# First value blocks of a hybrid attention step multiplied before their norm is known, first loads reordered, the sample's output block last but one

## The chip, the cores and the metric

The kernel runs on one core of a Trainium2 chip. Its time is the device time of one execution in microseconds, and the median of several runs counts. The engines named below are TensorE (PE in the profile; its weight loads are PEld), VectorE (DVE), ScalarE (ACT), GpSimd (POOL) and SyncE (SP), whose queue issues the transfers. A line number such as L213 is the line of the kernel file of before.

## The reference

One layer of a streaming encoder, for 1024 prompt frames and 32 frames of a running stream (the sample), each of 1024 channels. What matters here is how it starts and how it ends:

```python
def rmsnorm(x, g):
    xf = x.astype(F32)
    y = xf * lax.rsqrt(jnp.mean(xf * xf, axis=-1, keepdims=True) + EPS) * g.astype(F32)
    return y.astype(x.dtype)

def in_proj(xn, w_in, gla_w_a2, gla_b_a):
    u = xn @ w_in          # 1024 -> 10256 columns
    gq, gk, gv, gr, gg, dq, dk, dv, dg, ma, mb = jnp.split(u, IN_SPLITS, axis=-1)
    ...

def out_merge(x, o_gla, o_diff, gg, dg, ma, mb, ...):
    ...
    merged = jax.nn.sigmoid(ma) * (yg @ w_proj_gla) + jax.nn.sigmoid(mb) * (yd @ w_proj_diff)
    return x + rmsnorm(merged @ w_out, post_norm_g)
```

Between the two stand a gated linear attention of 4 heads and a differential attention of 8 heads, which the change doesn't touch. The factor of the root mean square is one number per frame, so it can be applied to the rows of x or to the rows of a product x @ w.

## The kernel before, in words

Every float32 product is made of three products of rounded parts: each operand is split into a high part (a copy rounded to the type fp32r, on ScalarE) and a low part (the operand less the high part, on VectorE, or on GpSimd for the projection weights), and high by high, low by high and high by low are added up in PSUM.

The normalized input stays in SBUF for the whole input projection: `X` holds 1024 channels (8 groups `k` of 128 partitions, kept as one tile of 6 groups and one of 2) by high and low part by 1056 frames. It is filled block by block; blocks 0 to 7 are 128 prompt frames each, block 8 is the sample's 32. For one block:

- `norm_square` (L196) loads the block twice, by rows (`xn`) and by columns (`xr`), takes the sum of squares of each row on ScalarE, and turns it into the factor, with a step on VectorE (L161) and a power on GpSimd (L162). Both tiles have two buffers.
- `norm_scale` (L210) spreads the factors over the partitions with a matmul (L213) into a bank of PSUM with the tag "t", of which there is one.
- `norm_apply` (L216) multiplies the columns by the norm's gain and the factor, eight times 128 columns on VectorE (L219), and copies the high part (L221, ScalarE); `norm_low` subtracts it (L225, VectorE).

While X is filled, TensorE multiplies it with the first of four quarters of the value weights (`value_weights`, four pieces of 512 KB, each loaded, copied and subtracted at L256, L258, L260). Block 0's product is written out by hand (`first`, L360) in the order in which its parts become ready. Block i from 1 on is 24 matmuls (`value_mm`, L285 to L287), and after the first six of them, in TensorE's order, stands `meanwhile`: the norm of block i+1, the load and squares of block i+2, and, for i from 3 to 6, a piece of the next weight quarter. `value_tile` (L268) evicts a finished product and stores it.

In this opening a block marked `manual_schedule` fixes the order of TensorE, ScalarE, VectorE and GpSimd as it is written. Operations from later parts of the program that are outside it (the split of the first projection weights, L433 and L435) may still be put between them by the planner, and the SP queue of transfers is ordered by the planner too. Warm-up matmuls (L335) run until the first data is there. From the second weight quarter on, everything reads X as it then stands.

At the end of the program the merged result is multiplied with `w_out`, in four column blocks `u` of 256, and within each over the blocks 0 to 8 (L1187). In the last column block each row block is also finished: a square sum of the last columns (L1204), the product with the gain (L1205), the sum (L1210), the power (L162), the scaling with the input added (L1213), and two stores (L1215). The sample's block has two more steps before these, since its two halves are added up from different partitions (L1200, L1201).

Of the kernel before, what the change touches and what calls it, by code (L numbers as in the profile page):

```python
# [11 lines left out]
F32 = mybir.dt.float32  # L12
# [3 lines left out]
ALU = mybir.AluOpType  # L16
# [106 lines left out]
def hybrid_step_kernel(ctx: ExitStack, tc: tile.TileContext, a):  # L123
# [71 lines left out]

    def norm_square(i):  # L196
        t0 = i * P
        w = P if i < NQ else NS
        xn = v1.tile([P, D], F32, tag="xn", bufs=2, name="xn")
        dma(xn[0:w], a["xn"][t0 : t0 + w, :])  # L200
        xr = v1.tile([P, KT, P], F32, tag="xr", bufs=2, name="xr")
        dma(xr[:, :, 0:w], a["xT"][i] if i < NQ else a["xTs"])
        if i == 0:
            dma(vecs, a["vecs"])
        s = ssx[0:w, i : i + 1]
        act(xn[0:w], xn[0:w], AF.Square, accum_out=s)
        rsqrt_mean(ssx[:, i : i + 1], w, 1, D)
        xrs[i] = xr

# [39 lines left out]

    def value_weights(u):  # L250
        wr = v1.tile([P, KT, 512], F32, tag="wr", name="wr")
        wh = v1.tile([P, KT, 512], F32R, tag="wh", bufs=2, name="wh")
        wl = v1.tile([P, KT, 512], F32R, tag="wl", bufs=2, name="wl")
        for k in range(0, KT, 2):
            k2 = slice(k, k + 2)
            dma(wr[:, k2], a["wv"][u, :, k2])  # L256
            yield wh, wl
            act(wh[:, k2], wr[:, k2], AF.Copy)  # L258
            yield wh, wl
            ve.tensor_tensor(wl[:, k2], wr[:, k2], wh[:, k2].bitcast(F32), op=ALU.subtract)  # L260
            yield wh, wl

    def value_tile(u, i, ps):
# [3 lines left out]
        if i < NQ:  # L267
            act(vo, ps, AF.Copy)  # L268
            st(dst[t0 : t0 + P, :], vo)
# [60 lines left out]
    with tc.manual_schedule(engines={E.PE, E.Activation, E.DVE, E.Pool}):  # L330

        def warm(n):
            ps = obank("ps_warm")
            for _ in range(n):
                mm(ps[:, 0:P], one_h, one_h, start=True, stop=True)  # L335
        warm(10)
        norm_square(0)
        s = norm_scale(0)
        warm(9)
        w0 = value_weights(0)  # L340

        def weights(n):
            for _ in range(n):
                wv = next(w0)
            return wv
        weights(2)
        norm_apply(*s, 0)
        weights(1)
        norm_low(*s, 0)
        weights(2)  # L350
        norm_apply(*s, 1)
        norm_low(*s, 1)
        weights(3)
        norm_square(1)
        wv = weights(3)
        ps = bank("ps_v")

        def first(p, ks):
            for k in ks:
                mm(ps, xs[k][:, p == 1, 0:P], wv[p == 2][:, k, :], start=(p == k == 0), stop=(p == 2 and k == KT - 1))  # L360
        first(0, range(6))
        first(1, range(6))
        s = norm_scale(1)
        norm_apply(*s, 0)
        weights(1)
        norm_apply(*s, 1)
        for p, ks in ((0, (6, 7)), (1, (6, 7)), (2, range(8))):
            first(p, ks)
        norm_low(*s, 0)
        norm_low(*s, 1)  # L370
        norm_square(2)
        w0 = value_weights(1)
        nxt = weights(1)
        for i in range(1, NQ + 1):
# [926 lines left out]
```

## Time and profile before

| | |
|---|---|
| median of 3 runs | 1483.13 us (1480.83 to 1486.48) |
| the profiled execution | 1483.59 us |
| its span, first to last instruction | 1481.9 us |
| TensorE busy | 1422.6 us, 96% |
| VectorE, ScalarE, GpSimd busy | 786.6, 601.0, 298.4 us |
| mean granted TensorE clock | 0.99 |
| moved by the DMA engines | 156.58 MB, 106 GB/s on average |

A row of the timeline gives the start and the duration in us, the engine, the line, the operation, what it writes and reads, and in brackets how long the engine stood idle before it and what ended that. A row of the groups gives the number of instructions, their busy time in us and the mean of one in ns. A busy share is an average over the whole span; for a change at one place, the rows of that place count.

### The profile page before, as it was taken

The numbers are of one execution on the slowest core, as the hardware profiler recorded it, in microseconds if no ns is written. First come the engines' busy times: TensorE is split into PE (matmuls) and PEld (weight loads), VectorE is DVE, ScalarE is ACT, GpSimd is POOL, SyncE is SP. The second block draws the span as 40 slices with busy tenths as digits, with TensorE's granted clock in tenths as the row PEclk, the third lists the DMA queues.
The fourth block names the chain that finished last, engine by engine and source line by source line (L and its number), as shares of the span: only waits on it lengthen the run. The fifth ranks groups of instructions, "written<-read, shape, count | busy, mean of one in ns | idle before, by whom it ended". The sixth has DMA issues, their size and how long they took to land.

```text
span 1481.9 us, 22365 instructions
## 1 busy us (share of the span) xinstructions
PE 1422.6 (96%) x8848; PEld 1327.6 (90%) x8848; DVE 786.6 (53%) x1464; ACT 601.0 (41%) x1262; POOL 298.4 (20%) x186
## 2 busy tenths in 40 slices
PE   8999999989999999899999999999899899999997
PEld 6787789889989899899989998998899799999997
DVE  5702005755565343576767767678665535455415
ACT  5612114535344232455555555555455432221311
POOL 1200002222213224123222222222221111122001
PEclk9999999999999999999999999999999999999999
DMA  8621111122222233323232333223322278633205
GB/s 310 205 105 38 45 45 48 56 74 68 81 70 73 70 120 108 90 62 106 72 108 60 106 86 96 69 83 90 92 68 81 97 264 302 223 131 129 103 1 192
DMA packets 66742, 156.58 MB, mean 106 GB/s; under 512 B 10008, under 2 KB 28568, under 8 KB 65600
## 3 DMA queue, kind: packets, MB, share of 16 engines
q1 hardware_dynamic: 66624, 155.01, 32.3%
q8 instruction: 74, 1.21, 0.3%
q14 instruction: 44, 0.36, 0.1%
HBM read 104.39 MB, written 40.04 MB: 97 GB/s over the span
## 4 chain that ended last, share of the span: by engine, by line
PE 51%; DVE 6%; DMA 4%; ACT 2%; issue 1%; POOL 1%; SPq 0%; DVEq 0%; POOLq 0%; ACTq 0%
PE ps_w L465 9%; PE ps_w L466 9%; PE ps_w L467 9%; PE ps_w L444 2%; PE ps_w L443 2%; PE ps_w L445 2%; PE ps_s L884 2%; PE ps_t L931 2%; PE ps_s L883 2%; DMA ydr<-ydd 2%; PE ps_c L1193 2%; PE ps_c L1195 2%; PE ps_c L1194 2%; PE po L945 1%; PE po L946 1%
## 5 line engine op out<-in xcount | busy, mean ns | idle before, releaser
L465 PE MATMUL ps_w<-X,wh 128*128 128x352 f32 x1344 | 453.8, 338 | 8.5 <-DVE sg L478 3.2
L466 PE MATMUL ps_w<-X,wl 128*128 128x352 f32 x1344 | 438.2, 326 | 0.0
L467 PE MATMUL ps_w<-X,wh 128*128 128x352 f32 x1344 | 436.4, 325 | 0.0
L435 POOL TENSOR_TENSOR wl<-wr,wh 128x1024 fp32r<-128x1024 f32 x72 | 179.5, 2493 | 661.8 <-ACT wh L433 528.6
L465 PEld LDWEIGHTS ps_w<-X,wh 128*128 128x128 f32 x1344 | 255.8, 190 | 13.6 <-issue 4.9
L466 PEld LDWEIGHTS ps_w<-X,wl 128*128 128x128 f32 x1344 | 256.1, 191 | 1.2 <-issue 1.2
L467 PEld LDWEIGHTS ps_w<-X,wh 128*128 128x128 f32 x1344 | 255.1, 190 | 0.0
L889 ACT ACTIVATE p<-ps_s,nm 128x256 f32<-128x256 f32 (+7 forms) x128 | 94.6, 741 | 59.1 <-DVE ps_s L885 31.1
L286 PE MATMUL ps_v<-wh,X 128*128 128x512 f32 x248 | 97.6, 393 | 0.6 <-DVE X L225 0.6
L287 PE MATMUL ps_v<-wl,X 128*128 128x512 f32 x248 | 98.0, 395 | 0.0
L433 ACT ACTIVATE wh<-wr 128x1024 fp32r<-128x1024 f32 x72 | 75.9, 1054 | 54.6 <-PE ps_w L467 30.4
L285 PE MATMUL ps_v<-wh,X 128*128 128x512 f32 x248 | 97.9, 395 | 0.0
L887 DVE TENSOR_REDUCE nm<-ps_s 128x1 f32<-128x256 f32 (+7 forms) x128 | 94.8, 747 | 2.7
L272 DVE TENSOR_TENSOR vo<-ps_v,vo 32x512 f32<-32x512 f32 x4 | 2.7, 679 | 139.9 <-ACT vo L271 139.9
L885 DVE MEMSET ps_s<- 64x64 f32 x128 | 14.3, 112 | 115.8 <-PE ps_s L884 114.2
L650 POOL TENSOR_TENSOR vl<-vr,vh 128x512 fp32r<-128x512 f32 (+1 forms) x20 | 24.8, 1242 | 222.8 <-DVE t L516 160.3
L883 PE MATMUL ps_s<-k,q 128*128 128x512 f32 (+2 forms) x192 | 68.0, 362 | 1.2 <-DMA k<-k 1.2
L884 PE MATMUL ps_s<-kl,q 128*128 128x512 f32 (+2 forms) x192 | 63.8, 348 | 3.9 <-DMA kl<-kl 3.4
L268 ACT ACTIVATE vo<-ps_v 128x512 f32<-128x512 f32 x32 | 19.1, 596 | 114.2 <-PE ps_v L287 113.8
L933 ACT ACTIVATE ah<-ps_t 128x512 fp32r<-128x512 f32 (+2 forms) x96 | 46.9, 488 | 43.6 <-PE ps_t L931 43.0
L934 DVE TENSOR_TENSOR al<-ps_t,ah 128x512 fp32r<-128x512 f32 (+2 forms) x96 | 53.1, 554 | 18.6 <-ACT ah L933 17.3
L444 PE MATMUL ps_w<-Y,wl 128*128 128x352 f32 x192 | 62.2, 324 | 0.0
(319 smaller groups left out, 2960.9 us busy)
## 6 DMA issues: line engine op xcount, KB each, us to landing
wr<-w SPq DMA_DIRECT2D x72, 512.0 KB
thd<-gate SPq DMA_DIRECT2D x16, 528.0 KB
xn<-xn SPq DMA_DIRECT2D x16, 512.0 KB
wr<-wv SPq DMA_DIRECT2D x16, 512.0 KB
newk<-rr SPq DMA_DIRECT2D x8, 528.0 KB
ygr<-ygd SPq DMA_DIRECT2D x8, 528.0 KB
tha<-thd SPq DMA_DIRECT2D x8, 528.0 KB
ydr<-ydd SPq DMA_DIRECT2D x8, 528.0 KB
```

The lines of the kernel that those rows point to most:

```text
L285: mm(ps, xk[:, 0, t0 : t0 + P], wh[:, k, :], start=(k == 0), stop=False)
L286: mm(ps, xk[:, 1, t0 : t0 + P], wh[:, k, :], start=False, stop=False)
L287: mm(ps, xk[:, 0, t0 : t0 + P], wl[:, k, :], start=False, stop=(k == KT - 1))
L435: nc.gpsimd.tensor_tensor(wl, wr, wh.bitcast(F32), op=ALU.subtract)
L444: mm(ps[:, :n], wl[:, k, :], src[k][:, 0, t0 : t0 + n], start=False, stop=False)
L465: mm(ps[:, :n], wh[:, k, :], src[k][:, 0, t0 : t0 + n], start=(k == 0), stop=False)
L466: mm(ps[:, :n], wl[:, k, :], src[k][:, 0, t0 : t0 + n], start=False, stop=False)
L467: mm(ps[:, :n], wh[:, k, :], src[k][:, 1, t0 : t0 + n], start=False, stop=(k == KT - 1))
L883: mm(ps[:, n0 : n0 + n], qs[m][:, qsl], ks[m][:, n0 : n0 + n], start=True, stop=False)
L884: mm(ps[:, n0 : n0 + n], qs[m][:, qsl], kls[m][:, n0 : n0 + n], start=False, stop=True)
L887: ve.tensor_reduce(nm, ps[:, 0:w], axis=AX.X, op=ALU.max, negate=True)
L889: act(p[:, 0:w], ps[:, 0:w], AF.Exp, bias=nm, accum_out=sm[:, m : m + 1])
```

## The change

1. **Blocks 0 and 1 are multiplied without the factor.** `raw_high` and `raw_low` split the columns times the gain alone, one group of 128 channels at a time: eight copies with a scale on ScalarE and eight operations on VectorE. Their products with the first weight quarter are scaled by the factor of each row as they are evicted (`value_tile`).
2. **X is put right afterwards.** In the value blocks 6 and 7, at the end of `meanwhile`, `raw_norm` normalizes blocks 0 and 1 in place: a matmul that spreads the factors into the bank "t", and for each of the two tiles of X an addition of high and low part, a product with the factors, a copy on ScalarE and a subtraction.
3. **The first loads are issued in another order**: the small vectors, the first piece of weights, the columns of block 0, the other three pieces, the columns of block 1, and then the rows of blocks 0 and 2; the columns of block 2 and the rows of block 1 follow when their buffers come free. The squares of blocks 0 and 2 are taken before the product of block 1, those of block 1 in its `meanwhile`, ahead of those of block 3.
4. **Block 0's product** is rewritten for pieces that arrive in that order; the low part of the third piece is made on GpSimd instead of VectorE. The warm-up is 15 matmuls in one run instead of 10 and 9.
5. **At the end**, the sample's block is multiplied last but one in each column block, and prompt block 7 last.

```diff
+    RAW = 2
+    def raw_high(i, ks):
+        for k in ks:
+            act(X[k // 6][:, k % 6, 0, i * P : i * P + P], xrs[i][:, k, :], AF.Copy, scale=g_pre[:, k : k + 1])
+    def raw_low(i, ks):
+        for k in ks:
+            x = X[k // 6][:, k % 6, :, i * P : i * P + P]
+            ve.scalar_tensor_tensor(x[:, 1], xrs[i][:, k, :], g_pre[:, k : k + 1], x[:, 0].bitcast(F32),
+                                    op0=ALU.mult, op1=ALU.subtract)
+    def raw_norm(i):
+        ps = tbank("ps_n")
+        mm(ps[:, 0:P], ssx[:, i : i + 1].to_broadcast([P, P]), ident, start=True, stop=True)
+        for x in X:
+            n = x.shape[1]
+            x = x[:, :, :, i * P : i * P + P]
+            t = v1.tile([P, KT, P], F32, tag="xr", bufs=2, name="xr")[:, 0:n]
+            ve.tensor_tensor(t, x[:, :, 0].bitcast(F32), x[:, :, 1].bitcast(F32), op=ALU.add)
+            ve.tensor_tensor(t, t, ps[:, 0:P].unsqueeze(1).to_broadcast([P, n, P]), op=ALU.mult)
+            act(x[:, :, 0], t, AF.Copy)
+            ve.tensor_tensor(x[:, :, 1], t, x[:, :, 0].bitcast(F32), op=ALU.subtract)
...
-            act(vo, ps, AF.Copy)
+            if u == 0 and i < RAW:
+                act(vo, ps, AF.Copy, scale=ssx[:, i : i + 1])
+            else:
+                act(vo, ps, AF.Copy)
...
+        warm(15)
+        wr, wh, wl = wv = value_tiles()
+        dma(vecs, a["vecs"])
+        for n in range(4):
+            dma(wr[:, 2 * n : 2 * n + 2], a["wv"][0, :, 2 * n : 2 * n + 2])
+            if n == 0:
+                load_cols(0)
+        load_cols(1)
+        xn0, xn2 = load_rows(0), load_rows(2)
...
+        high(0)
+        raw_high(0, range(4))
+        low(0)
+        raw_low(0, range(4))
+        first(0, (0, 1))
+        first(1, (0, 1))
+        first(2, (0, 1))
+        high(1)
+        raw_high(0, range(4, 8))
+        low(1)
+        raw_low(0, range(4, 6))
...
+        high(2)
+        low(2, nc.gpsimd)
+        raw_low(0, range(6, 8))
+        first(0, (4, 5))
+        first(1, (4, 5))
+        high(3)
+        low(3)
+        for p, ks in ((0, (6, 7)), (1, (6, 7)), (2, (4, 5, 6, 7))):
+            first(p, ks)
+        raw_high(1, range(8))
+        raw_low(1, range(8))
+        square(0, xn0)
+        load_cols(2)
+        square(2, xn2)
+        xn1 = load_rows(1)
...
             def meanwhile():
                 norm_tile(i + 1)
+                if i == 1:
+                    square(1, xn1)
                 if i < NQ - 1:
                     norm_square(i + 2)
                 if i in (3, 4, 5, 6):
                     weights(3 if i < 6 else 2)
+                if i > 5:
+                    raw_norm(i - 6)
...
-        for i in range(NQ + 1):
+        for n, i in enumerate((*range(NQ - 1), NQ, NQ - 1)):
...
-            ps = (bank, dbank)[i % 2]("ps_c")[:, 0:256]
+            ps = (bank, dbank)[n % 2]("ps_c")[:, 0:256]
```

`load_rows`, `load_cols` and `square` are the parts of the former `norm_square`; in `first`, pass 0 is high by high, pass 1 low by high, pass 2 high by low.

More of the change, by code (lines that the diff above doesn't have):

```diff
@@ L335, in warm, with high, low, first @@
                 mm(ps[:, 0:P], one_h, one_h, start=True, stop=True)
[L336 to L340, printed above, removed]
+        warm(15)
[7 more added lines that the diff above has]
+        xn0, xn2 = load_rows(0), load_rows(2)
+        def high(n):
+            k2 = slice(2 * n, 2 * n + 2)
+            act(wh[:, k2], wr[:, k2], AF.Copy)
+        def low(n, eng=ve):
+            k2 = slice(2 * n, 2 * n + 2)
+            eng.tensor_tensor(wl[:, k2], wr[:, k2], wh[:, k2].bitcast(F32), op=ALU.subtract)
+        ps = bank("ps_v")
+        def first(p, ks):
+            for k in ks:
+                mm(ps, xs[k][:, p == 1, 0:P], wv[1 + (p == 2)][:, k, :], start=(p == k == 0), stop=(p == 2 and k == KT - 1))
+        high(0)
[9 more added lines that the diff above has]
+        raw_low(0, range(4, 6))
+        first(0, (2, 3))
+        first(1, (2, 3))
+        first(2, (2, 3))
+        high(2)
[13 more added lines that the diff above has]
+        xn1 = load_rows(1)
+        wv = wv[1:]
+        w0 = value_weights(1)
         def weights(n):
@@ L345, in weights @@
             return wv
[L346 to L372, printed above, removed]
         nxt = weights(1)
```

29 lines of the change are left out of this document (18 added, 11 removed).

## The prediction

> **What bounds the kernel now.** I read the page first, then the timeline of the first 66 us engine by engine, the groups of that stretch by shape, and the last 20 us.
>
> ```profile
> span 1481.9 us, 22365 instructions
> PE 1422.6 (96%) x8848; PEld 1327.6 (90%) x8848; DVE 786.6 (53%) x1464; ACT 601.0 (41%) x1262; POOL 298.4 (20%) x186
> PE   8999999989999999899999999999899899999997
> ```
>
> TensorE is busy for 96% of the span; only the first and the last of the 40 slices are clearly short of full. The change edits just these two, so what it can win is TensorE's idle time there, and what it adds between them costs only where TensorE is made to wait. In the opening, ScalarE (columns: start, duration, engine, line, operation) shows when loads land, since it waits for them:
>
> ```profile
> 4.69 1.06 ACT L206 ACTIVATE xn<-xn 128x1024 f32<-128x1024 f32 x1 [2.61 <-DMA xn<-xn]
> ...
> 8.19 1.06 ACT L258 ACTIVATE wh<-wr 128x1024 fp32r<-128x1024 f32 x1 [2.34 <-DMA wr<-wv]
> ...
> 14.93 1.06 ACT L258 ACTIVATE wh<-wr 128x1024 fp32r<-128x1024 f32 x1 [0.61 <-DMA wr<-wv]
> ```
>
> The rows of block 0 are the first 512 KB load (landed 4.69), the first weight piece is the third (8.19), the last piece the eighth (14.93): 1.75 us per load, then 1.35. TensorE in the same stretch, with the engines that hold it:
>
> ```profile
> 10.03 0.74 PE L360 MATMUL ps_v<-wh,X 128*128 128x512 f32 x2 [0.74 <-ACT X L221]
> ...
> 19.46 0.73 PE L360 MATMUL ps_v<-wl,X 128*128 128x512 f32 x2 [0.56 <-DVE wl L260]
> ...
> 22.29 0.49 PE L213 MATMUL ps_n<-ident,ssx 128*128 128x128 f32 x2
> ...
> 22.81 2.16 DVE L219 SCALAR_TENSOR_TENSOR xr<-xr,vecs,ps_n 128x128 f32<-128x128 f32 x8 [1.21 <-PE ps_n L213]
> ...
> 27.21 0.55 POOL L162 TENSOR_TENSOR ssx<-ssx,mhalf 128x1 f32<-128x1 f32 x1 [1.29 <-DVE ssx L161]
> ...
> 28.20 0.38 PE L213 MATMUL ps_n<-ident,ssx 128*128 128x128 f32 x2
> ```
>
> Block 0's 24 matmuls take from 10.03 to 20.2. From the norm matmul of block 2 (22.29) to that of block 3 (28.20) a block costs 5.91 us: with some 0.3 for the norm matmul, 0.234 a matmul, 5.6 for 24. So block 0 is 4.5 us longer than its work, and it starts 10 us late.
>
> **The opening, step by step.** Loads now go: vectors, weight piece 0, columns of block 0, pieces 1 to 3, columns of block 1, rows of blocks 0 and 2. With the pitch read above and half a microsecond for the small load put first, they land at 5.2, 6.9, 8.7, 10.0, 11.4, 12.7, 14.0 and 15.4 (estimates). The splits cost:
>
> ```profile
> L260 DVE TENSOR_TENSOR wl<-wr,wh 128x1024 fp32r<-128x1024 f32 x8 | 9.8, 1223 | 3.0 <-ACT wh L258 3.0
> L225 DVE TENSOR_TENSOR X<-xr,X 128x768 fp32r<-128x768 f32 x8 | 8.7, 1093 | 2.4 <-ACT X L221 2.4
> ...
> L933 ACT ACTIVATE ah<-ps_t 128x128 fp32r<-128x128 f32 x16 | 4.4, 277 | 5.5 <-PE ps_t L931 5.5
> ```
>
> A 128x128 raw_high has no row: above it is the nearest, L933, with 0.277, and below it an eighth of the 1024-column L258, 0.13. I take 0.22, nearer to L933, whose shape it has. raw_low is priced as L219, eight in 2.16 us, 0.27 each. ScalarE: piece 0 from 5.2 to 6.3, four raw_high to 7.8, piece 1 from 8.7 to 9.7, four more to 10.6, piece 2 to 11.6, piece 3 to 12.6, eight raw_high of block 1 to 14.5, the two squares (1.06 and a read of the accumulator) to 15.7 and 16.9. TensorE starts at about 7.2. The low part of piece 2 is now on GpSimd, and there two engines hold each other:
>
> ```profile
> 14.43 1.21 DVE L260 TENSOR_TENSOR wl<-wr,wh 128x1024 fp32r<-128x1024 f32 x1
> 14.59 1.46 POOL L162 TENSOR_TENSOR ssx<-ssx,mhalf 128x1 f32<-128x1 f32 x1 [7.85 <-DVE ssx L161]
> ...
> 47.35 2.43 POOL L435 TENSOR_TENSOR wl<-wr,wh 128x1024 fp32r<-128x1024 f32 x1 [2.25 <-ACT wh L433]
> ...
> 48.96 1.64 DVE L225 TENSOR_TENSOR X<-xr,X 128x768 fp32r<-128x768 f32 x1 [0.40 <-ACT X L221]
> ```
>
> The 0.55 us power took 1.46 because a VectorE subtraction of two SBUF tiles had begun 0.16 earlier and ended at 15.64; the subtraction at 48.96 took 1.64 against the mean of 1.09 of its shape, since GpSimd's ended only at 49.78. So the two don't share: the later one starts when the earlier ends. [...] If engines overlapped freely instead, the low part would be hidden and the opening would end as in the upper bound below.
>
> GpSimd's piece 2 is the L435 shape: 2.43 us. VectorE is done with piece 1 at 11.0 and with block 0's last raw_low at 12.0; GpSimd gets in there, to 14.5. Piece 3's low part (1.22), ready at 12.6, runs from 14.5 to 15.7, block 1's eight raw_low to 17.8, then the mean steps and two powers (0.55 each) to 19.2. Block 0 ends at 16.2 on TensorE instead of 20.2. But the norm matmul of block 2 stands after six matmuls of block 1, at 17.5, and its power, behind all that VectorE work, is done at 19.2: TensorE waits, and goes on at 19.3 instead of 22.29, 3.0 earlier. What is late next: block 1's square, inserted ahead of block 3's, adds 1.15 us on ScalarE; block 3's power was done at 27.76, 0.44 before its matmul at 28.20, so 0.7 goes back. **Opening: -2.3.** Bounds: if GpSimd loses each race and starts after block 1's raw_low (at 16.0), the low part comes at 18.4, block 0 ends at 19.4 and the norm matmul of block 2 stands at 20.8, 1.5 earlier than before, less the same 0.7: -0.8. If nothing collides and nothing waits after, block 2's square at 16.9 sets its power to 17.8: -4.5. Scaling at the eviction is the same activation with a scale, hidden under the 5.6 us of the next block's matmuls, into another bank; the two norm matmuls saved there lie in the times above.
>
> **The two blocks normalized later.** raw_norm runs in the value blocks 6 and 7, after six matmuls, right behind the norm matmul of blocks 7 and 8 (the sample). Its matmul writes a bank of the tag "t", of which there is one, and TensorE keeps its order. VectorE there, before:
>
> ```profile
> 52.40 2.15 DVE L219 SCALAR_TENSOR_TENSOR xr<-xr,vecs,ps_n 128x128 f32<-128x128 f32 x8
> ...
> 57.23 1.23 DVE L260 TENSOR_TENSOR wl<-wr,wh 128x1024 fp32r<-128x1024 f32 x1 [0.81 <-ACT wh L258]
> 58.38 1.35 DVE L219 SCALAR_TENSOR_TENSOR xr<-xr,vecs,ps_n 128x32 f32<-128x32 f32 x8
> ```
>
> VectorE reads the bank about 0.5 us after the norm matmul starts (22.29, 22.81), so that matmul stood at 51.9 and 57.9. All in the clock of before:
> - Block 6: the raw matmul waits until the eight reads end at 54.55; with 0.25 of its own, matmuls go on at 54.85 instead of 52.1: +2.75. The 18 matmuls behind it wait.
> - Block 7: the sample's norm matmul comes at 60.6, but the bank is held by raw_norm(0): VectorE ends L260 at 58.46, adds 768 columns (0.9, three fourths of L260), multiplies (0.95), waits for ScalarE's copy (three fourths of L258 and the hand-over, 0.95), subtracts (0.9), and adds and multiplies the 256 columns of the small group (0.4 each): 62.95. +2.4.
> - Then raw_norm(1)'s matmul waits for the small group's copy and subtraction (0.8) and the sample's eight multiplies (1.35): 65.1 where matmuls would go on at 63.2, and 0.25 of its own: +2.2.
>
> **Sum of this part: +7.35.** VectorE's last 5 us of raw_norm(1) lie under the sample and the next weight block. Bounds: +4.75, where raw_norm(0) is over before block 7 needs the bank (2.75, and 1.35 + 0.65); +9.8, where one GpSimd split of 2.43 falls into this chain, as it fell onto 48.96.
>
> **The end.**
>
> ```profile
> 1464.09 0.39 ACT L1204 ACTIVATE sqj<-ps_c 128x256 f32<-128x256 f32 x1 [2.24 <-PE ps_c L1195]
> ...
> 1466.03 1.41 DVE L1213 SCALAR_TENSOR_TENSOR ogb<-ogb,s,xn 128x512 f32<-128x512 f32 x2 [0.73 <-POOL s L162]
> ...
> 1474.01 0.38 ACT L1200 ACTIVATE tl<-ps_c 32x256 f32<-32x256 f32 x1 [1.28 <-PE ps_c L247]
> ...
> 1477.57 1.40 DVE L1213 SCALAR_TENSOR_TENSOR ogwwl<-ogwwl,s,xn 32x512 f32<-32x512 f32 x2 [0.72 <-POOL s L162]
> ```
>
> TensorE ends at 1474.0 either way. From there the sample needs 4.96 us to the end of L1213 (1478.97), a full block 3.35 (1464.09 to 1467.44): 1.6 less. But the sample's own L1213 (1.4) can stand before the last block's on VectorE, which leaves 0.2; and the last stores are 128 rows instead of 32, 256 KB against 64 each, 0.5 more at the 1.35 us per 512 KB of the loads. Between -1.1 and +0.3, and as nothing tells which L1213 goes first, the middle: **-0.4**.
>
> **The sum** goes against the profiled execution, 1483.59 us (its span and 1.7 around it), 0.46 above the median 1483.13: 1483.59 - 2.3 + 7.35 - 0.4 = **1488.2**. The 1400 us between start by TensorE's progress; I take them as shifted whole.
>
> **Rivals.** *Both ends kinder:* nothing collides at the opening (-4.5), raw_norm(0) is over in time (+4.75), the end gives its 1.1: 1482.7. For it: VectorE stands idle for 0.81 before L260 in the quoted stretch. Against it: the chain of 4.5 us after 58.46 doesn't fit before 60.6. *The bank isn't waited for* (raw_norm's matmul is placed elsewhere): two pairs of matmuls cost 0.5, so 1481.4, or 1478.5 with the kinder opening and end. Against it: each norm matmul stands where the code has it. *Slower:* a GpSimd split of a projection weight, not in the hand-written order, falls between 52 and 65 us into VectorE's chain and holds it for 2.43; with a lost race at the opening and the longer end: 1483.59 - 0.8 + 9.8 + 0.3 = 1492.9. It decides from the point where that split starts after 52.4 instead of 47.35; an opening shorter by 2 us alone moves it the other way, but its load and copy may shift.
>
> **Chances.** The forecast 0.55 (its own range 1485.5 to 1490.5), both ends kinder 0.17, no wait 0.10, slower 0.18. The range 1479.5 to 1492.5 leaves out half of the slower rival and the best of the no-wait one. Half a per cent (7.4 us) is about what a measurement of this kernel can tell from no change: the bounds are 1475.7 and 1490.5. Faster 0.03, from no wait with all else at its best; slower 0.20, the slower rival and the upper edge of the forecast; same 0.77.
>
> **What would show it.** The first value matmul near 7.2; block 0's end near 16; a wait of TensorE for block 2's power. A GpSimd subtraction near 12 with VectorE idle beside it. In blocks 6 and 7, three waits of TensorE's norm matmuls for VectorE, 2.75, 2.4 and 2.2. The last VectorE operation nearer than 5 us to the last matmul. No such waits in blocks 6 and 7, or an opening shorter by over 5 us, would make the prediction wrong.

## The result: slower by 1.1%

| | before | after |
|---|---|---|
| median | 1483.99 us (6 runs, 1480.83 to 1489.53) | 1500.57 us (6 runs, 1497.70 to 1505.54) |
| ratio | | 1.0113, 95% interval 1.0086 to 1.0139 |
| profiled execution, its span | 1483.59, 1481.9 us | 1497.70, 1496.0 us |
| mean granted TensorE clock | 0.990 | 0.987 |

The change costs 16.6 us in the median and 14.1 us between the two profiled spans. The forecast was +4.6 (1488.2 us, range to 1492.5), so the median lies 8 us above the range. The head of the page after the change:

```profile
span 1496.0 us, 22381 instructions
PE 1425.8 (95%) x8840; PEld 1329.3 (89%) x8840; DVE 793.6 (53%) x1471; ACT 605.8 (40%) x1278; POOL 300.5 (20%) x187
PE   8899999898999899899999999999899989999997
```

TensorE has 8 matmuls less and is busy 3.2 us longer: the same work takes more time, besides the waits. The opening slice has become no fuller. Lines moved by the edit: L213 is now L246, L219 L252, L225 L258, L285 to L287 are L325 to L327, L360 L397, L435 L500, L579 L644, L622 L687, L1213 L1278.

**The opening.** The timeline after, with the rows that answer those shown of before:

```profile
7.32 1.59 PE L397 MATMUL ps_v<-wh,X 128*128 128x512 f32 x4
...
11.32 2.40 POOL L392 TENSOR_TENSOR wl<-wr,wh 128x1024 fp32r<-128x1024 f32 x1 [9.69 <-ACT wh L388]
...
12.22 2.58 DVE L392 TENSOR_TENSOR wl<-wr,wh 128x1024 fp32r<-128x1024 f32 x1 [0.79 <-ACT wh L388]
...
18.23 0.49 PE L246 MATMUL ps_n<-ident,ssx 128*128 128x128 f32 x2 [1.25 <-POOL ssx L162]
...
24.07 1.06 ACT L209 ACTIVATE xn<-xn 128x1024 f32<-128x1024 f32 x1 [1.45 <-DMA xn<-xn]
...
26.09 0.49 PE L246 MATMUL ps_n<-ident,ssx 128*128 128x128 f32 x2 [1.77 <-POOL ssx L162]
```

TensorE's first value matmul starts at 7.32, the norm matmul of block 2 at 18.23 instead of 22.29, that of block 3 at 26.09 instead of 28.20. GpSimd's split from 11.32 to 13.72 held VectorE's, which took 2.58 instead of 1.22, as argued. What gives most of the time back at block 3 is a load: its rows were issued (18.77) behind the store of block 0's values (18.41), and ScalarE waited 1.45 us for them. That store in turn stood behind the eviction with the scale, which couldn't start before block 0's factor was there (17.69, when its last matmuls had been over for 2 us).

**Blocks 6 and 7.** Before, the first split of a projection weight and the eviction of the sample's values stood here (the second split, at 47.35, is shown ahead):

```profile
23.52 2.40 POOL L435 TENSOR_TENSOR wl<-wr,wh 128x1024 fp32r<-128x1024 f32 x1 [1.29 <-ACT wh L433]
...
66.38 0.59 ACT L271 ACTIVATE vo<-ps_v 32x512 f32<-32x512 f32 x1 [3.09 <-PE ps_v L247]
```

After, from 52 us on:

```profile
53.01 2.38 POOL L500 TENSOR_TENSOR wl<-wr,wh 128x1024 fp32r<-128x1024 f32 x1 [2.37 <-ACT wh L498]
...
54.15 0.49 PE L233 MATMUL ps_n<-ident,ssx 128*128 128x128 f32 x2 [2.84 <-DVE xr L252]
...
60.15 2.42 POOL L500 TENSOR_TENSOR wl<-wr,wh 128x1024 fp32r<-128x1024 f32 x1 [2.94 <-ACT wh L498]
...
60.84 2.54 DVE L241 TENSOR_TENSOR X<-xr,X 128x768 fp32r<-128x768 f32 x1 [0.91 <-ACT X L240]
...
64.44 0.37 PE L246 MATMUL ps_n<-ident,ssx 32*128 32x32 f32 x2 [2.66 <-DVE xr L239]
...
66.53 0.79 PE L233 MATMUL ps_n<-ident,ssx 128*128 128x128 f32 x2 [1.71 <-DVE xr L252]
...
77.39 0.59 ACT L311 ACTIVATE vo<-ps_v 32x512 f32<-32x512 f32 x1 [3.09 <-PE ps_v L280]
```

The three waits are there, 2.84, 2.66 and 1.71 us (2.75, 2.4 and 2.2 were forecast; that the second came out so near is luck, as experiment 1 shows). But the sample's rows are evicted at 77.39, where they were at 66.38: +11.0, and not 5. Two things came on top. GpSimd's projection weight splits (L500) now start at 53.01 and 60.15 instead of 23.52 and 47.35, and the subtraction L241, forecast at 0.9 and 0.96 long at 69.91 without a split beside it, takes 2.54 beside the second. And TensorE's clock fell. Busy time by stretch, after the change (columns: stretch, its length, then busy time and count of PE, PEld, DVE, ACT and POOL, granted TensorE clock, DMA share, GB/s):

```profile
24.06:27.47 3.41, 1.64 (x9) 1.20 (x8) 1.01 (x5) 1.72 (x3) 0.55 (x1) 1.00 0.97 365
27.47:30.88 3.41, 3.41 (x10) 2.63 (x9) 2.75 (x9) 2.19 (x4) 0.14 (x1) 0.50 0.92 299
...
51.37:54.78 3.41, 0.63 (x4) 0.59 (x5) 3.02 (x10) 2.23 (x4) 1.77 (x1) 1.00 0.47 124
54.78:58.19 3.41, 3.41 (x10) 2.64 (x9) 3.22 (x5) 1.97 (x3) 1.14 (x2) 0.50 0.48 142
...
61.60:65.01 3.41, 0.56 (x3) 0.29 (x2) 2.86 (x4) 0.68 (x2) 0.97 (x1) 1.00 1.02 406
65.01:68.42 3.41, 1.89 (x6) 1.60 (x7) 3.19 (x13) 0.80 (x3) 1.41 (x4) 0.50 0.54 139
68.42:71.83 3.41, 3.41 (x10) 2.64 (x9) 2.30 (x4) 0.97 (x2) 2.61 (x8) 0.50 0.29 115
```

In these rows each stretch of 3.41 us in which TensorE was busy for 1.9 us or less is followed by one at half clock. The half-clock stretches from 27.47, 54.78 and 68.42 have 10 matmuls; those from 30.88 and 71.83, at 1.00, have 17 and 16. There are four stretches at half clock before 72 us; in the profile of before there is none.

**The first head.** A second loss lies far from the edit. Between the first projection matmul of the state stage (L465 before; 218.16 to 229.17, +11.0) and the last matmuls of the heads' output product (L700 before; 550.87 to 568.51, +17.6) another 6.6 us go, although TensorE's and VectorE's instructions stand there in the same order. At the first branch (the exact path, which is jumped over on these inputs) VectorE's timeline before:

```profile
262.83 0.18 DVE L570 TENSOR_TENSOR ar<-ps_as,causal 32x32 f32<-32x32 f32 x1 [1.37 <-PE ps_as L569]
264.14 1.23 DVE L622 TENSOR_TENSOR b<-b 128x1024 f32<-128x1024 f32 x1 [1.13 <-DVEq L579]
```

and after:

```profile
274.34 0.18 DVE L635 TENSOR_TENSOR ar<-ps_as,causal 32x32 f32<-32x32 f32 x1 [1.37 <-PE ps_as L634]
279.47 1.23 DVE L687 TENSOR_TENSOR b<-b 128x1024 f32<-128x1024 f32 x1 [4.95 <-DVEq L644]
```

VectorE's own queue, and no other engine, holds it for 4.95 us instead of 1.13. The waits over the four heads (columns: what waited for what, us in total, times, longest), before and after:

```profile
DVE b L622 <- DVEq L579: 8.9, 4, 3.6
```

```profile
DVE b L687 <- DVEq L644: 15.5, 4, 5.0
```

**The end.** The sample's scaling comes ahead of the last block's on VectorE:

```profile
1488.52 1.40 DVE L1278 SCALAR_TENSOR_TENSOR ogwwl<-ogwwl,s,xn 32x512 f32<-32x512 f32 x2 [0.72 <-POOL s L162]
...
1491.24 1.41 DVE L1278 SCALAR_TENSOR_TENSOR ogwwl<-ogwwl,s,xn 128x512 f32<-128x512 f32 x2 [0.73 <-POOL s L162]
```

From the first output matmul to the end of the span it takes 103.3 us (1392.67 to 1496.0), before 103.5 (1378.36 to 1481.9).

### The profile page after: what moved, and what is told of

Same layout as the page of the kernel before. It is cut to its first block, busy times and chain, and to the rows that moved or that the text cites. A ratio compares the mean times of both kernels' runs of the same rounds, so it can differ in the third digit from the quotient of the medians.

```text
span 1496.0 us, 22381 instructions
## 1 busy us (share of the span) xinstructions
PE 1425.8 (95%) x8840; PEld 1329.3 (89%) x8840; DVE 793.6 (53%) x1471; ACT 605.8 (40%) x1278; POOL 300.5 (20%) x187
## 4 chain that ended last, share of the span: by engine, by line
PE 50%; DVE 6%; DMA 4%; ACT 2%; issue 1%; POOL 1%; SPq 0%; DVEq 0%; POOLq 0%; ACTq 0%
PE ps_w L530 9%; PE ps_w L531 9%; PE ps_w L532 9%; PE ps_w L509 2%; PE ps_w L508 2%; PE ps_w L510 2%; PE ps_s L949 2%; PE ps_t L996 2%; PE ps_s L948 2%; PE ps_c L1258 2%; PE ps_c L1259 2%; PE ps_c L1260 2%; DMA ydr<-ydd 1%; DMA kl<-kl 1%; PE po L1010 1%
## 5 line engine op out<-in xcount | busy, mean ns | idle before, releaser
L500 POOL TENSOR_TENSOR wl<-wr,wh 128x1024 fp32r<-128x1024 f32 x72 | 179.4, 2492 | 666.4 <-ACT wh L498 520.7
L327 PE MATMUL ps_v<-wl,X 128*128 128x512 f32 x248 | 100.2, 404 | 0.0
L325 PE MATMUL ps_v<-wh,X 128*128 128x512 f32 x248 | 100.0, 403 | 0.0
L326 PE MATMUL ps_v<-wh,X 128*128 128x512 f32 x248 | 99.5, 401 | 0.0
```

The source lines that it names most:

```text
L325: mm(ps, xk[:, 0, t0 : t0 + P], wh[:, k, :], start=(k == 0), stop=False)
L326: mm(ps, xk[:, 1, t0 : t0 + P], wh[:, k, :], start=False, stop=False)
L327: mm(ps, xk[:, 0, t0 : t0 + P], wl[:, k, :], start=False, stop=(k == KT - 1))
L500: nc.gpsimd.tensor_tensor(wl, wr, wh.bitcast(F32), op=ALU.subtract)
```

## The experiments

The table gives, for every profiled execution, when a stage's end stands against the profile of before, in us. L465 is the first projection of the state stage, L700 the output product of its four heads (lines of before); the heads' column is the difference of the two beside it; the waits are VectorE's behind the four branches.

| kernel | sample's values evicted | first L465 | last L700 | heads | four waits | output stage | span |
|---|---|---|---|---|---|---|---|
| before | 66.38 | 218.16 | 550.87 | | 8.9 | 103.5 | 1481.9 |
| after | +11.0 | +11.0 | +17.6 | +6.6 | 15.5 | 103.3 | +14.1 |
| fillers | +7.6 | +7.6 | +12.4 | +4.8 | 15.3 | 104.5 | +7.8 |
| banks | +7.9 | +8.7 | +15.3 | +6.6 | 15.5 | 104.1 | +12.4 |
| shift 256 | +9.4 | +10.2 | +9.0 | -1.2 | 8.8 | 106.9 | +9.9 |
| before, shift 10, new tile | | +2.3 | +6.6 | +4.2 | 14.6 | 106.5 | +6.3 |
| before, output order | | +3.2 | +4.4 | +1.2 | 8.8 | 103.8 | +1.6 |
| deferred | 0.0 | +2.3 | +7.6 | +5.3 | 14.8 | 103.8 | +4.2 |
| before, shift 56 | | +2.0 | +3.2 | +1.1 | 9.8 | 106.5 | +6.2 |
| deferred and mended | -1.9 | -1.0 | -1.5 | -0.5 | 9.2 | 106.9 | +0.7 |
| before, new tile only | | +4.2 | +2.9 | -1.3 | 9.0 | 106.5 | +5.4 |
| before, shift 10 only | | +6.2 | +13.1 | +6.9 | 15.4 | 103.5 | +13.0 |
| before, short branch | | +0.8 | -2.9 | -3.7 | 3.9 | 103.5 | -7.1 |
| all together | -1.6 | -0.1 | -4.3 | -4.1 | 3.9 | 103.8 | -6.9 |

How far one profile may be trusted is read from the kernels that leave the value stage as it was before (the six whose second column is empty): their first L465 stands 0.8 to 6.2 us later than in the profile of before, which is the quickest of its kind there; their value matmuls follow each other at 0.2309 to 0.2333 us, and some have a half-clock stretch in the opening. So a few us in that column are chance, the medians decide on totals, and what lies inside a stage is read from its own rows.

**1. Fillers ahead of the five waits** (after, changed)

```
+ warm({1: 4, 2: 6, 7: 10}.get(i, 0))   # ahead of norm_tile(i + 1)
...
+ warm({6: 11, 7: 6}[i])                # ahead of raw_norm(i - 6)
```

> The changed kernel with dependency-free filler matmuls (results never read) on TensorE just ahead of the norm matmuls that were seen to wait: 4 ahead of block 2's norm, 6 ahead of the third's, 11 ahead of raw_norm(0)'s, 10 ahead of the sample's, 6 ahead of raw_norm(1)'s. They fill the waits, so TensorE does not stand idle there. Theory C (half of the loss in the value stage is the granted clock, which falls to 0.50 after each of these waits): no slice at 0.50 between 26 and 75 us, the sample's block is evicted near 72.6 us instead of 77.4 (-4.7), the total near 1496 (-4.7 against the changed kernel). Rival V (VectorE's chain sets these times and the clock only follows): the norm matmuls start where they did, the sample's eviction stays at 77 +- 1 us, total 1500 +- 1.

Three of the four half-clock stretches are gone:

```profile
27.47:30.88 3.41, 3.41 (x17) 2.79 (x16) 2.31 (x7) 2.77 (x5) 0.55 (x1) 1.00 0.86 305
...
54.78:58.19 3.41, 3.41 (x18) 2.83 (x17) 2.99 (x3) 1.29 (x2) 0.51 (x2) 1.00 0.66 205
```

Block 3's norm matmul comes at 25.65, the one for block 7 at 48.94 (after 50.92, before 51.91): the opening's gain of 3.0 is whole. The sample's rows are evicted at 73.98, 3.4 earlier: neither the 4.7 of theory C nor nothing. From raw_norm(0)'s matmul to the sample's norm it takes 10.2 us without the half clock and 10.3 with it (52.08 to 62.28, and 54.15 to 64.44): there VectorE's chain sets the time.

```profile
57.90 2.39 PE L377 MATMUL ps_warm<-one_h 128*128 128x128 f32 x20
62.28 0.37 PE L246 MATMUL ps_n<-ident,ssx 32*128 32x32 f32 x2 [1.98 <-DVE xr L239]
62.58 2.60 PE L377 MATMUL ps_warm<-one_h 128*128 128x128 f32 x12
64.97 0.63 PE L233 MATMUL ps_n<-ident,ssx 128*128 128x128 f32 x2
```

TensorE is through with its work at 57.90 and could go on at 62.28: the second wait, fillers included, is 4.4 us. It looked like 2.66 in the changed kernel because the matmuls ahead of it ran slowly. The fourth half-clock stretch stays (62.98 to 66.39). In it the last fillers run past the point where VectorE's reads end (64.31), so that raw_norm(1)'s matmul starts 0.7 late, and the first matmuls behind it lose another 0.6. So the clock is worth 3.4 of the 11.0 as measured, and some 4.6 with these 1.2, an estimate from these rows. The median, 1498.06 us, is 2.5 below that of after, within the scatter of both.

**2. Other banks for raw_norm** (after, changed)

```
- ps = tbank("ps_n")
+ ps = (obank, dbank)[i]("ps_n")
```

> The changed kernel with the two accumulators of raw_norm taken from the banks of the tags o and s, which nothing else uses in these blocks, instead of from the tag t, where they wait for the eight split reads (L252) of the norm before. Nothing else differs. Theory B (the wait for the bank is the cost): raw_norm's matmuls start without a wait, the sample's norm is reached some 9 to 11 us earlier and its block is evicted near 66 to 68 us instead of 77.4; total 1490 +- 1.5. Rival V (the order of the work on VectorE is the cost: the sample's norm_apply stands behind raw_norm(0) there and cannot start earlier): the wait moves from raw_norm's matmul to the sample's own matmuls, the eviction is at 73 to 75.5 us; total 1497.5 +- 1.

raw_norm's matmuls no longer wait (49.92 and 58.61). The wait moved, as rival V has it, to the sample's first product, which needs GpSimd's pairing, which needs the sample's low part, which stands behind raw_norm(0) on VectorE:

```profile
49.92 0.28 PE L233 MATMUL ps_n<-ident,ssx 128*128 128x128 f32 x1
...
67.48 0.69 PE L276 MATMUL ps_v<-wh,xsm 128*64 128x512 f32 x1 [4.18 <-POOL xsm L271]
```

The eviction is at 74.26 (73 to 75.5 expected), the median 1496.38. The bank is only the first thing that shows; the work on VectorE is the price.

**3 and 4. VectorE's instructions moved by 246, and by 10**

```
+ padt = cst.tile([P, 1], F32, name="padt")
...
+ for _ in range(246):        # in after; 10 of them in before
+     ve.memset(padt, 0.0)
```

> The changed kernel with 246 memsets of one element per partition on VectorE in the third value column block, where VectorE has idle time. They leave every result as it was; they only shift the place of VectorE's later instructions, so that with the 10 that the change adds it is 256 instructions beyond where it stood in the kernel before. Theory P (the first branch on VectorE, L579 before and L644 after, resumes late because of the place of its instructions: 0.5 us from the branch to the next event before, 4.4 us after): VectorE's instruction behind the first branch waits 1.1 to 1.5 us instead of 4.95, the four branches together 9 instead of 15.5, and the shift against the kernel before does not grow from 11 to 17 across the first head; total 1494.5 +- 1.5 (-4 to -7). Rival (the late resumption follows from the later start of the stage, or from the clock): total as the changed kernel's, 1500.5 +- 1.

> The kernel before with 10 memsets of one element per partition on VectorE in the third value column block: the same count of VectorE instructions ahead of the first branch as the change adds, and nothing else of the change. Theory P: the wait at VectorE's first instruction behind the first branch grows from 1.1 to about 5 us, the time between the first product of the state stage and the first output projection of the first head grows by 4 to 6 us; total 1489 +- 1.5 (+4 to +7). Rival: 0, total 1484 +- 1.

They weren't executed where they are written: the planner put the 246 between 1.2 and 93.2 us, the 10 between 1.2 and 2.3. The place of the branches in VectorE's instructions moves all the same. In the first, VectorE resumes behind the first branch after 1.13 us again, and the heads take 1.2 us less than before instead of 6.6 more; median 1496.25. In the second, the kernel before has the late branches of after (4.52, 3.12, 3.47 and 3.51 us, together 14.6) and its heads take 4.2 longer. Its median, 1492.84, is 9.4 above before, more than theory P has: the output stage is 3 us longer as well (106.5). Both kernels with `padt` show that; in the first it takes 106.9 us and hides part of the gain.

**5. The output order alone** (before, with the last hunk of the diff)

> The kernel before with the last part of the change alone: in the output stage the sample's block is written last but one instead of last. From the profiles of before and after: the loop on TensorE ends 0.8 us earlier behind its first matmul, the stretch from TensorE's end to the end of the span grows by 0.6; sum -0.3 (from -1.0 to +0.6). If the last part is worth nothing, neither number moves; if the sample's own scaling on VectorE delays the last block by more than its 1.2 us, the sum is above +0.6. The total of one run can't show this; the markers can.

The output stage takes 103.8 us, against 103.5 before and 103.3 after. The other kernels with this order and no new tile have 103.8 to 104.5, all three with the old order 103.5: between -0.2 and +1.0, so no gain that shows. The one run, 1485.22 us, tells no more.

**6. raw_norm deferred** (after, changed)

```
- if i > 5:
-     raw_norm(i - 6)
...
+ order = (*range(2, NQ + 1), 0, 1)     # second column block, written by hand
...
+ # in meanwhile of its second and third block:
+ raw_norm(n - 1)
```

The load of the gate's weights and the products with them move along with the second column block.

> The changed kernel with raw_norm's work moved out of blocks 6 and 7: block 0 and block 1 are normalized behind the sample's block, while TensorE works on the second value column block, whose order is 2 to 7, sample, 0, 1 so that the two come last. The unnormalized opening and the output order stay. Theory: the 11 us of the value stage are the price of raw_norm's place, not of the unnormalized products; without it the sample's block is evicted 0.5 to 3 us earlier than in the kernel before (66.38), so at 63.4 to 65.9, and the first product of the state stage starts that much earlier as well; the late first branch (VectorE stands 13 instructions beyond the kernel before) still costs 5; total 1487 +- 2. Rival: the normalization has no place where it is free, VectorE and ScalarE then hold the second column block up and the first product of the state stage is 5 us or more later than before; total 1494 or more.

The median is 1489.94 us, 10.6 below that of after: the place of raw_norm is the larger part of the loss. In its new place its two matmuls (73.11 and 78.94) wait for nothing, and the one wait of TensorE in the second column block and behind it is 0.46 us, for a sum of the gate's low rank at 120.6. The ratio to before is still 1.0051 (1.0031 to 1.0071), and the four branches are late (14.8). What was not expected: the sample's eviction, at 66.36, is no earlier than before, although block 3's norm was 1.8 earlier and block 7's 2.1. GpSimd's timeline of this kernel:

```profile
59.37 2.43 POOL L515 TENSOR_TENSOR wl<-wr,wh 128x1024 fp32r<-128x1024 f32 x1 [2.16 <-ACT wh L513]
62.08 1.48 POOL L271 CAST xsm<-X 128x64 fp32r<-128x64 f32 x8 [0.28 <-DVE X L258]
```

The projection weights, loaded later in this order, are split at 59.37; the sample's subtraction (L258, 32 columns, 0.5 us without company) takes 2.58 beside it, and the pairing on GpSimd starts at 62.08, where it started at 60.27 before. The opening's gain is given back there.

**7. Shift by 56** (before, with 58 one-element copies behind the last weight split)

> The kernel before with 58 one-element copies on VectorE behind the last weight split, where VectorE waits for the sample for 40 us, so that its later instructions stand 56 further. Theory P, with a period of 128 instructions (8 KB, one packet of the queue that was seen just ahead of the late resumption): of the four branches the first and third are late now and the second and fourth are not, the opposite of the kernel before: waits of VectorE behind them 4.5, 1.1, 3.5, 1.0 us (before: 1.13, 3.17, 1.00, 3.58). Rival (only the shift by 10 to 20 or a period of 256 matters): some other pattern, or the waits of the kernel before.

The waits are 4.55, 0.87, 3.47 and 0.94: the pattern of theory P with a period of 128. First and second branch:

```profile
269.73 1.23 DVE L625 TENSOR_TENSOR b<-b 128x1024 f32<-128x1024 f32 x1 [4.55 <-DVEq L582]
...
333.18 1.22 DVE L625 TENSOR_TENSOR b<-b 128x1024 f32<-128x1024 f32 x1 [0.87 <-DVEq L582]
```

**8. Deferred and mended** (the deferred kernel, changed)

```
+ xn1, xn3 = load_rows(1), load_rows(3)
...
+ warm({1: 4, 2: 3}.get(i, 0))          # ahead of norm_tile(i + 1)
...
+ for _ in range(112 if u == 3 else 0): # padt is a new tile
+     ve.tensor_copy(padt, wv[1].bitcast(F32)[:, 0, 0:1])
```

> The deferred kernel (raw_norm behind the sample's block) with three more edits: the rows of the fourth block are loaded ahead of the first store of values, 4 and 3 filler matmuls bridge the waits ahead of the norms of blocks 2 and 3, and 112 one-element copies on VectorE behind the last weight split put its branches 124 instructions beyond the kernel before. Theory: no half-clock slice between 16 and 40 us; block 3's norm at 24.2 to 25 us (before 28.20), the sample's block evicted at 62 to 63.5 (before 66.38); the first branch resumes in 1.1 us as before (128 being the period), with no growth of the distance across the first head; end -0.3; total 1480 +- 1.5 (-3 to -5 against before). Rival: opening and branch are bought back later by transfers, total 1484 +- 1.

Block 3's norm stands at 25.08, the sample's eviction at 64.52, the branches resume as before (1.13, 3.15, 0.98, 3.91). The output stage takes 106.9. Median 1484.38, ratio 1.0007 (0.9997 to 1.0018): opening and branch are won, but 3.4 us are lost at the end; every kernel with `padt` loses 3.0 to 3.4 there. About as much is missing to the expected 1480.

**9. The new tile alone** (before, changed)

```
+ padt = cst.tile([P, 1], F32, name="padt")
+ nc.gpsimd.memset(padt, 0.0)
```

> The kernel before with one more tile of 4 bytes per partition among the constants, written once by GpSimd and read by nobody; no instruction of VectorE, ScalarE or TensorE is added. The four earlier kernels with such a tile (it held the one-element memsets and copies) all ran the output stage at 0.1187 us per matmul, the six without it at 0.1136 to 0.1148. Theory A (the tile moves the addresses of what lies behind it, and TensorE reads some operand of the output stage more slowly there): 0.1186 per matmul from the first to the last of the 768, the stage 3.1 us longer, total 1486.5 +- 1.5. Rival (chance, or VectorE's instructions): 0.1146, total 1483.3 +- 1.5.

Theory A's figures hold in the stage (that it is an address isn't shown): 0.1186 us from matmul to matmul, 106.5 us in all. The median is 1488.11, ratio 1.0042 (1.0025 to 1.0058), 5.3 above before where 3.1 were expected; what is beyond the stage's 3.0 isn't explained by it. The same 8 us of the output stage, 56 us behind its first matmul, before:

```profile
1434.40:1442.40 8.00, 8.00 (x73) 8.00 (x72) 1.27 (x3) 1.43 (x6) 0.00 (x0) 1.00 0.01 2
```

and with the tile:

```profile
1436.80:1444.80 8.00, 8.00 (x69) 8.00 (x68) 0.89 (x3) 1.28 (x6) 0.00 (x0) 1.00 0.01 2
```

At the same granted clock of 1.00, and with TensorE never idle, 69 matmuls go where 73 went.

**10. Shift by 10 without a new tile** (before, with 11 copies into `lp`, a tile no longer used)

> The kernel before with 11 one-element copies on VectorE behind the last weight split, written into a tile that is already there and no longer used, so that no address moves; VectorE's first branch is its instruction 216, as in the changed kernel (206 before). Theory P alone: waits behind the four branches 4.5, 3.2, 3.5, 3.6 us, total +4 to +6 (1488.5 +- 1.5); the output stage runs at 0.1146 us per matmul. Rival: what the first such experiment showed (+9.4) was all the tile's, total 1484 +- 1.

Branches late (5.00, 3.29, 3.60, 3.52), heads 6.9 longer, output stage 103.5, median 1490.40, ratio 1.0056 (1.0039 to 1.0074): +7.6 where 4 to 6 were expected. The code's place alone costs the kernel before about what it costs the changed one.

**11. A shorter branch** (before, changed)

```
- ve.tensor_tensor(dst[:, :ncol], dst[:, :ncol], src[:, :ncol], op=ALU.mult)
+ nc.gpsimd.tensor_tensor(dst[:, :ncol], dst[:, :ncol], src[:, :ncol], op=ALU.mult)
...
- ve.tensor_tensor(ar[0:w, c, 0:w], ar[0:w, c, 0:w], tm[0:w, 0:w], op=ALU.add)
+ nc.gpsimd.tensor_tensor(ar[0:w, c, 0:w], ar[0:w, c, 0:w], tm[0:w, 0:w], op=ALU.add)
...
+ # and 40 one-element copies into lp behind the last weight split
```

> The kernel before with a shorter branch on VectorE: in the exact path, which is jumped over on these inputs, the products with q and k and the sums of the masked parts are given to GpSimd, so that VectorE's jump is 158 instructions long instead of 233; 40 one-element copies into an unused tile behind the last weight split put the four branches at 116, 104, 103 and 99 of 128. Theory P with the figure that a late resumption belongs to a jump that ends two blocks of 128 on: all four branches resume early, waits 0.9 to 1.1 us each; the distance over the four heads is 3 to 5 us shorter; total 1479.5 +- 1.5. Rival: the later branches' waits were covered by TensorE's fill work, total 1483 +- 1.

All four branches resume early:

```profile
DVE b L624 <- DVEq L581: 3.9, 4, 1.1
```

The heads are 3.7 us shorter, but the median of 12 runs is 1482.23, ratio 0.9996 (0.9981 to 1.0010): the waits are gone as theory P has it, but the total is the rival's, and a gain in it cannot be told from nothing. Why the heads' 3.7 us don't arrive in the median stays open. The profiled execution, 1476.54, is the fastest of the twelve.

**12. All together** (deferred, the earlier load, fillers of 4 and 3, the shorter branch, 157 copies into `lp`)

> The deferred kernel with the earlier load of the fourth block's rows, the fillers of 4 and 3 matmuls, the shorter branch, and 157 one-element copies into an unused tile (no new tile, so no address moves). Theory, from the sums so far: opening -1 at the first projection of the state stage (measured in the kernel like it), output stage at 0.1146 per matmul again (-3.1 against that kernel), four early branches (-4); total 1477.5 +- 2, faster than the kernel before by 0.2 to 0.5%. Rival: 1481 or more, if the branches' gain does not reach the end.

```profile
span 1475.0 us, 22582 instructions
PE 1421.1 (96%) x8854; PEld 1325.3 (90%) x8854; DVE 820.7 (56%) x1628; ACT 605.6 (41%) x1278; POOL 300.2 (20%) x187
```

The median of 12 runs is 1478.15 us, against 1482.80 for before on the same chip: ratio 0.9971 (0.9958 to 0.9984), faster than both kernels, by 4.7 us and by some 21. It stands within its expectation. How the gain divides among its edits isn't shown: the short branch alone moved the median by 0.6.

## Why the prediction was wrong

**Adding up.** Against their own runs of before, after is +16.6, the deferred kernel +6.7, and the kernel before with nothing but VectorE's instructions moved by 10 is +7.6. So raw_norm's place costs about 10, the place of VectorE's code about 7, and what remains of the change (the opening and the output order) comes to about -1, with an uncertainty of 3 or more.

**"Opening: -2.3."** Right in its mechanism. The first matmul was forecast at 7.2 (7.32), the low part on GpSimd with VectorE held (2.58 instead of 1.22), block 0's end at 16.2 (its last matmuls start at 14.85), block 2's norm at 19.3 (18.23). The 0.7 given back at block 3 was 1.9 (-4.1 to -2.1): 1.45 of it is ScalarE's wait for a load behind a store in SP's queue, for which the prediction has no term, and the rest fits the order on ScalarE that it named. With that load issued ahead (experiments 8 and 12) block 3's norm follows block 2's by 6.59 and 6.81 us, 0.7 and 0.9 above the 5.91 of before. What failed is the end of the step: that a block which starts earlier stays earlier. The wait of 1.77 halved the clock for 3.4 us, and at block 4's norm 0.5 was left (33.56 instead of 34.02); with the fillers 2.5 is left there, and 3.0 at block 7's. The prediction has no term for the clock; every wait in it was priced at its own length.

**"Sum of this part: +7.35."** The path through VectorE's chain was right (the single bank is only where it shows first, as experiment 2 has it), and the term was too small. The three waits measure 7.2 together in the changed kernel, but that they come so near is luck: the slow matmuls hid part of the second. With the fillers the stretch from block 7's norm to the sample's eviction is 10.6 longer than before (48.94 to 73.98, against 51.91 to 66.38), above the upper bound of 9.8. About 1.2 of this is the half-clock stretch that stays there, so some 9.4 are left (an estimate), 2 above the forecast. 1.5 of the 2 fit the second split of a projection weight: L241 takes 2.43 beside it in this run (2.54 in the changed kernel), and 0.95 without. The other 0.5 is that VectorE turns to block 7's norm 0.94 us behind its matmul, where it took 0.49. The prediction held such a split as its slower rival, with the condition that it starts after 52.4: one started at 53.01 and one at 60.15. (The rival's 1492.9 is still short of the result, since it has neither the clock nor the code's place.) The first costs this chain nothing: L258 takes 2.04 beside it instead of 1.29, but VectorE then still stands idle for 0.19 until ScalarE is done. No run was made without the splits, so this is read from the rows and not shown by an experiment; what the deferred kernel shows is that such a split holds up the sample there too. The other bound, that the bank wait could go elsewhere at 0.5, falls: with free banks only 3.1 us of the eviction's 11.0 are saved.

**"The 1400 us between ... I take them as shifted whole."** This is the step with the largest error. It holds for data and order, and not for the place of the code: the change adds 10 VectorE instructions ahead of the first branch. The reading that only the first and the last slice are short of full was wrong too: the quoted row has an 8 in five slices, the first being one of them, and the one from 296 to 333 us lies among the heads, around the late second branch of before (329.65). In the six kernels whose branches all stand in a late place (waits of 14.6 to 15.5 us) the heads take 4.2 to 6.9 us longer than before, in the five with waits of 8.8 to 9.8 between 1.3 less and 1.2 more, in the two with 3.9 about 4 less. Moving the instructions alone, by 10 in the kernel before or by 246 in the changed one, makes and unmakes it.

**"The end: -0.4."** Within its bounds, and nothing: -0.2 in the profile of after, +0.3 in the order's own run.

Behind the heads the profile's terms then add up: +5.05 as forecast (-2.3 and 7.35), -0.7 since the opening's gain is 3.0 while the clock is kept up, some 4.6 for the clock, 2.0 for the split and VectorE's later start, and 6.6 for the code's place, 17.6 in all; +17.6 was measured. At the end it is +14.1: 3.3 us are gained between the heads and the output stage. Of these, 0.9 and 1.4 fall at 602 and 1039 us, where the profile of before has half clock for 6.83 and 3.41 us and the one of after for 3.41 (at 621) and not at all. The other kernels stand between 0.1 later and 5.6 earlier than before on that stretch, so it is this one profile of before that is slow there, and not the change that gains.

## What to carry to other kernels

Price a wait of TensorE by what it does to the clock of the next few microseconds (here 3.41 us or more at half clock behind waits of 1.7 to 2.8), and bridge a wait that can't be removed with matmuls nobody reads, few enough that they end with the wait (in experiment 1 a matmul started 0.7 us late behind fillers that ran past it). Work taken off one engine's opening has to be put where the engine that receives it has room, not where its operands first become free; here, one column block later, TensorE waited for none of it. Before believing or discarding a change of under 1%, look at what moved without being edited: a branch's place in the instruction stream (+7.6 us in experiment 10) and, by the reading of experiment 9 (+5.3), the addresses of tiles allocated after a new one.

## What the runs showed of the hardware

**A stretch need not be idle to halve the clock.** The records of the granted clock change only on a grid of 3.413 us: in the profiles of before and after every full record lasts a whole number of such steps, one or two of them at half clock. I set TensorE's busy time (the ends of matmuls are modelled) in each such stretch of the 14 profiles, but for the first and the last 20 us, against the clock of the next. Below 1.5 us busy, 57 of 58 were followed by half clock; from 1.5 to 2.0, 19 of 65; from 2.0 to 3.25, 14 of 646; above, none of 5165. In the changed kernel waits of 1.7 to 2.8 us were enough. The grid doesn't start with the kernel (a mark of it lies 4.97 us into the span of before and 7.00 into that of after, 2.03 apart), so I take it as chance where a wait falls in it, and that may be part of the 0.8 to 6.2 us by which unchanged value stages differ.

**A branch's price depends on its place.** In the 14 profiles VectorE passes 56 branches: 20 resume after 0.86 to 1.13 us, 36 after 3.12 to 5.07. Ahead of each of the 36 by 1.9 to 2.4 us, and of none of the 20 at that distance, starts an instruction packet of 8 KB of one queue (14); the transfers after the change between 277.3 and 277.6, 2 us ahead of the row at 279.47 (columns: queue and kind, packets, MB, share), hold one:

```profile
q14 instruction: 1, 0.01, 6.4%
```

Counting VectorE's instructions modulo 128, the period that experiment 7 bears out, jumps over 233 of them were early from positions 69 to 87 and late from 88 on and through 43; jumps over 158 were early from the positions tried, 99 to 119. One rule tells all 56 apart: if the blocks of 128 begin at 65 of this count (fitted, not read), every early jump ends one block on and every late one two. That a late branch waits for the packet of 8 KB ahead of it is my reading of these times, not shown by a run; what is measured is its price, 2 to 4 us. That 128 instructions fill 8 KB is an estimate, at 64 bytes each: in the profile of before packets of 16 KB of queue 8 start at 24.1, 53.0, 82.3, 110.6 and 136.9 us, and from one to the next TensorE runs 126 to 129 matmuls and 125 to 128 weight loads.

**Four bytes cost 3 us.** A tile of 4 bytes per partition, allocated ahead of others, slows the output stage's 768 full matmuls from 0.1136 to 0.1148 us apart to 0.1186 or 0.1187, at a granted clock of 1.00, in all five kernels that had it and in none of the nine without. That it is the addresses of the tiles behind it is the reading that fits, since nothing else of TensorE's, VectorE's or ScalarE's program differs in the kernel with the tile alone; whether an operand is read more slowly there, and which, isn't shown.

**GpSimd and VectorE hold each other** where both subtract in SBUF, as read before the change: beside a split of GpSimd VectorE's subtraction took 2.58 us for 1.22 (12.22), 2.54 for 0.96 (60.84, against 69.91), 2.58 for 0.5 in the deferred kernel.
